# Rank-scatter of rows: early loads as one DMA of 10 KB packets, and two more thin groups

## The chip, the cores and the metric

The kernel runs on one core of one Trainium2 chip. The metric is device microseconds (us) of one execution. The record numbers the chip of each batch of experiments: chip 1 for the first batch (here B1), chip 9 for the second (B2), chip 2 for the last (C). The chip of the first comparison isn't recorded (here "chip A"; it could be one of the others). Three of the four first runs of the kernel before, and its trace, were taken earlier and stand under A too.

## The reference

```python
B, N, D = 8, 2048, 2560          # x: [B, N, D] float32 (168 MB), scores: [B, N] float32
order = np.argsort(scores, axis=1)
ranks = np.argsort(order, axis=1)
out[b_idx, ranks, :] = x         # row i of batch b goes to row ranks[b, i]
```

Each row of 10 KB is moved once, unchanged. The work is to find the ranks (a little arithmetic) and to move 168 MB in and 168 MB out.

## The kernel before

Ranks are counted on VectorE. The rows are cut into groups of 256 (128 partitions x 2 rows). Most groups are loaded to SBUF and scattered to their ranks by GpSimd's indirect DMAs, both on queue q0. Six groups (the first of batches 0 to 5) go another way: SP and ACT issue, per row, one DMA from DRAM to DRAM whose 10 KB go as 16 packets of 640 bytes ("row copies", queues q1 and q10; the trace of before has 25216 such packets for 1576 rows).

A "thin" group takes 4 partitions out of a group: their rows are made out of bounds for the scatter (by adding N to their rank), sometimes for the load too, and go by row copies. One DMA engine serves the four at 48-51, so a thin group there lightens that engine.

```python
GROUPS = [(256 * i, 2) for i in range(8)]
BULK = [(b, g) for b in range(B) for g in range(len(GROUPS)) if g or b not in DIRECT]   # 58 buffers
NBUF, LAG = 8, 4
THIN = {**{(b, 4): 48 for b in range(1, B, 2)}, (7, 5): 44}   # (batch, group): first partition
THIN_LOADS = [k for k in THIN if k[0]]
HALVED = range(34)                                             # loads split into 10 KB packets

def load(line, k, sem):
    ...   # a thin load: indirect DMA in which 4 partitions are out of bounds
    rows = x[b, r:r + P * m, :].rearrange("(p j) d -> p (j d)", j=m)
    for j in range(m if k in HALVED else 1):
        part = slice(j * D, (j + 1) * D) if k in HALVED else slice(0, m * D)
        line.eng.dma_start(out=xb[k % NBUF][:, part], in_=rows[:, part]).then_inc(sem, 16)
...
# row copies, 16 to a loop on SP and on ACT:
for i in range(G):
    line.eng.dma_start(out=out_bytes[bass.ds(at[i], ROW)],
                       in_=x_bytes[bass.ds(q * (G * ROW) + (first + i) * ROW, ROW)]).then_inc(s_rows[line], 16)
...
# GpSimd's loop:
for k, (b, g) in enumerate(BULK):
    if k >= LAG and k + NBUF - LAG < len(BULK):
        scatters_done(pl, k - LAG)          # the buffer is free
        load_ahead(k + NBUF - LAG)
    pl.wait(*loaded[k])
    pl.after(dve, t_bulk[b, g])             # the ranks are there
    for j in range(GROUPS[g][1]):
        scatter(k, j)                       # one indirect DMA per column: 128 rows
```

Of the kernel before, what the change touches and what calls it, by code (L numbers as in the profile page):

```python
# [40 lines left out]
def kernel(  # L41
# [6 lines left out]
    nc = tc.nc  # L48
# [18 lines left out]



    THIN = {**{(b, 4): 48 for b in range(1, B, 2)}, (7, 5): 44}  # L70
    HOLES = sorted(set(THIN.values()))

    THIN_LOADS = [k for k in THIN if k[0]]

    HALVED = range(34)

    STEPS = [(0, 1), (1, 2), (2, 4), (4, 8)]

# [16 lines left out]
    hole = pool.tile([P, len(HOLES)], F32, name="hole")  # L95
    below = pool.tile([P, 1], F32, name="below")
    thin_row = pool.tile([P, len(HOLES)], I32, name="thin_row")
    thin_i = {k: pool.tile([1, 4 * MMAX], I32, name=f"thin_i{k[0]}_{k[1]}") for k in THIN}
    rows_i = {b: pool.tile([1, WIDE], I32, name=f"rows_i{b}") for b in DIRECT}
    xb = [pool.tile([P, MMAX * D], F32, name=f"x{i}") for i in range(NBUF)]  # L100
    ps_col = psum.tile([P, 512], F32, name="ps_col")
# [7 lines left out]
    with tc.tile_critical(no_gpsimd_drain=True):  # L109
# [5 lines left out]
        s_scores = nc.alloc_semaphore("scores")  # L115
        s_first = nc.alloc_semaphore("first")
        s_load = [nc.alloc_semaphore(f"load{i}") for i in range(NBUF)]
        s_scat = [
            [nc.alloc_semaphore(f"scat{i}_{j}") for j in range(MMAX)]
            for i in range(NBUF)  # L120
        ]
        s_rows = {sp: nc.alloc_semaphore("rows_sp"), act: nc.alloc_semaphore("rows_act")}
        n_scat = [[0] * MMAX for _ in range(NBUF)]

        n_load = [0] * NBUF
        t_thin = []
# [1 line left out]
        def load(line, k, sem):  # L128
            b, g = BULK[k]
            r, m = GROUPS[g]  # L130
            if (b, g) in THIN_LOADS:

                i = HOLES.index(THIN[b, g])
                line.after(dve, t_thin[0])
                nc.gpsimd.indirect_dma_start(  # L135
                    out=xb[k % NBUF][:, :m * D],
                    out_offset=None,
                    in_=x.rearrange("b (q j) d -> (b q) (j d)", j=m),
                    in_offset=bass.IndirectOffsetOnAxis(ap=thin_row[:, i:i + 1], axis=0),
                    element_offset=(b * N + r) * D,  # L140
                    bounds_check=P - 1,
                    oob_is_err=False,
                ).then_inc(sem, 16)
                n_load[k % NBUF] += 1
                return
            rows = x[b, r:r + P * m, :].rearrange("(p j) d -> p (j d)", j=m)
            for j in range(m if k in HALVED else 1):
                part = slice(j * D, (j + 1) * D) if k in HALVED else slice(0, m * D)
                line.eng.dma_start(  # L149
                    out=xb[k % NBUF][:, part], in_=rows[:, part]  # L150
                ).then_inc(sem, 16)
                if k:
                    n_load[k % NBUF] += 1


        sp.eng.dma_start(out=s_in[:], in_=scores).then_inc(s_scores, 16)
        load(sp, 0, s_first)
        loaded = {0: (s_first, 16 * (2 if 0 in HALVED else 1))}


        t_zero = pl.did(nc.gpsimd.memset(ident[:], 0.0))
# [88 lines left out]
        def ranks(b, g_lo, g_hi):  # L250

            for g in range(g_lo, g_hi):
                lo = first_col(g)
                m = GROUPS[g][1]
                for j in range(m):
                    col = b * C + lo + j
                    score = s_col[:, lo + j, b:b + 1]
                    dve.after(dve, dve.n)

                    def count(i, lo_c, hi_c, do, **how):  # L260
                        dve.did(
                            do(  # L262
                                out=trash[i][:, :P * (hi_c - lo_c)],
                                in0=s_all[:, P * lo_c:P * hi_c],
                                accum_out=acc[i][:, col:col + 1],
                                **how,
                            )
                        )

                    count(  # L270
                        0, lo, C, nc.vector.tensor_scalar,
                        scalar1=score, scalar2=None, op0=OP.is_lt, op1=OP.add,
                    )
                    if lo:
                        count(
                            1, 0, lo, nc.vector.tensor_scalar,
                            scalar1=score, scalar2=None, op0=OP.is_le, op1=OP.add,
                        )
                    count(
                        2, lo, lo + m, nc.vector.scalar_tensor_tensor,  # L280
                        scalar=score,
                        in1=mask[:, MMAX - j:MMAX - j + m, :].rearrange("p a b -> p (a b)"),
                        op0=OP.is_equal, op1=OP.mult,
                    )
            cols = slice(b * C + first_col(g_lo), b * C + first_col(g_hi))
            dve.after(dve, dve.n)
            dve.did(
                nc.vector.tensor_tensor(  # L288
                    out=rank[:, cols], in0=acc[0][:, cols], in1=acc[1][:, cols], op=OP.add
                )  # L290
            )
            dve.after(dve, dve.n)
            dve.did(
                nc.vector.tensor_tensor(  # L294
                    out=rank[:, cols], in0=rank[:, cols], in1=acc[2][:, cols], op=OP.add
                )
            )
            dve.after(dve, dve.n)
            tick = dve.did(
                nc.vector.tensor_copy(out=rank_i[:, cols], in_=rank[:, cols])  # L300
            )
            for g in range(g_lo, g_hi):
                t_bulk[b, g] = tick
                if (b, g) in THIN:
                    cols = slice(b * C + first_col(g), b * C + first_col(g + 1))
                    i = HOLES.index(THIN[b, g])
                    dve.after(dve, dve.n)
                    t_bulk[b, g] = dve.did(
                        nc.vector.tensor_scalar(  # L309
                            out=rank_i[:, cols],  # L310
                            in0=rank[:, cols],
                            scalar1=hole[:, i:i + 1],
                            scalar2=None,
                            op0=OP.add,
                        )
                    )
# [11 lines left out]
                )  # L328

        def thin_to_bytes(b, g):  # L330
            m = GROUPS[g][1]
            dve.after(pe, pe.n)
            t_rows[b, g] = dve.did(
                nc.vector.tensor_scalar(  # L334
                    out=thin_i[b, g][:].rearrange("o (j i) -> o j i", j=m),
                    in0=ps_row[:1, :P * m].rearrange("o (j p) -> o j p", j=m)[
                        :, :, THIN[b, g]:THIN[b, g] + 4
                    ],
                    scalar1=float(b * N),
                    scalar2=float(ROW),  # L340
                    op0=OP.add,
                    op1=OP.mult,
                )
            )
# [63 lines left out]
        def thin_rows(n, b, g):  # L408
            line, name = ((sp, ENG.SP), (act, ENG.Activation))[n % 2]
            r, m = GROUPS[g]  # L410
            line.after(dve, t_rows[b, g])
            _, at = nc.values_load_multi_w_load_instructions(
                thin_i[b, g][:],
                engines=[name],
                min_val=b * N * ROW,
                max_val=(b * N + N - 1) * ROW,
                skip_runtime_bounds_check_because=(
                    "a rank counts other scores of one batch of N, so it lies in 0..N-1"
                ),
            )  # L420
            for i in range(4 * m):
                row = b * N + r + (THIN[b, g] + i % 4) * m + i // 4
                line.eng.dma_start(
                    out=out_bytes[bass.ds(at[i], ROW)],
                    in_=x_bytes[bass.ds(row * ROW, ROW)],
                ).then_inc(s_rows[line], 16)
                n_rows[line] += 1
# [37 lines left out]


        def scatters_done(line, k):
            i = k % NBUF
            for j in range(GROUPS[BULK[k][1]][1]):
                line.wait(s_scat[i][j], 16 * n_scat[i][j])  # L470

        def scatter(k, j):
            b, g = BULK[k]
            col = b * C + first_col(g) + j
            n_scat[k % NBUF][j] += 1
            nc.gpsimd.indirect_dma_start(  # L476
                out=out_flat,
                out_offset=bass.IndirectOffsetOnAxis(ap=rank_i[:, col:col + 1], axis=0),
                in_=xb[k % NBUF][:, j * D:(j + 1) * D],
                in_offset=None,  # L480
                element_offset=b * N * D,
                **(dict(bounds_check=N - 1, oob_is_err=False) if (b, g) in THIN else {}),
            ).then_inc(s_scat[k % NBUF][j], 16)

        def load_ahead(k):
            i = k % NBUF
# [47 lines left out]
```

## Time and profile before

| | before |
|---|---|
| median of 4 runs (chip A) | 772.09 us (770.55 to 772.5) |
| span of the profiled run | 769.8 us |
| VectorE / GpSimd / TensorE busy | 52% / 22% / 4% |
| bytes in DMA packets, mean rate | 319.74 MB, 415 GB/s |
| q0 packets, share of 16 engines | 29376, 92.0% |
| row copies (SP / ACT) | 792 / 784 |

A share of "16 engines" is the time that the packets of a queue took, over 16 times the span. The lines themselves are in the prediction below. One more view of before, the waits of SP's own queue:

```profile
SPq L109 <- DMA out_dram<-in_x_dram: 27.7, 1, 27.7
...
SPq L109 <- POOLq L109: 11.1, 1, 11.1
```

The columns are total us, number of waits, longest. The first is SP's wait, after it has issued its last row copy, until all its copies have landed. The second is how long SP then waits for GpSimd, thus for the scatters. Read the second as the slack of SP's row copies: they are done 11.1 us before the rest.

### The profile page before, as it was taken

What the parts mean: (1) busy time and instruction counts of PE and PEld (TensorE: products, weight loads), DVE (VectorE), ACT (ScalarE), POOL (GpSimd) and SP (SyncE); (2) the same over time, 40 slices, a digit from 0 to 9 for tenths busy, and PEclk for the clock granted to TensorE, in tenths of its full rate; (3) what the DMA queues carried; (4) which work ended last, traced back from release to release, by engine and by line L of the source; (5) the groups of instructions that cost most, each with busy time, mean ns of one, the idle gap of its engine ahead of it and who ended that gap; (6) DMA issues with size and microseconds to landing.
All of it is one profiled execution on the core that took longest, in us unless ns stands there. A gap on an engine that the chain in (4) does not pass through costs nothing.

```text
span 769.8 us, 8160 instructions
## 1 busy us (share of the span) xinstructions
PE 33.4 (4%) x166; PEld 29.2 (4%) x166; DVE 400.1 (52%) x824; ACT 0.0 (0%) x1; POOL 167.1 (22%) x213
## 2 busy tenths in 40 slices
PE   4000020020020020110000000000000000000000
PEld 4000010010010010110000000000000000000000
DVE  5999979999979999899999200000000000000000
ACT  0000000000000000000000000000000000000000
POOL 4114214312213131221212121212112121312100
PEclk8555555555555555565555555555555555555555
DMA  8999999999999999999999999999999999999997
GB/s 356 420 419 418 418 421 417 417 419 419 418 417 417 416 419 417 419 419 418 417 418 418 425 417 423 417 422 419 422 417 423 419 420 422 419 425 416 426 411 332
DMA packets 80130, 319.74 MB, mean 415 GB/s; under 512 B 28580, under 2 KB 53796, under 8 KB 53796
## 3 DMA queue, kind: packets, MB, share of 16 engines
q0 software_dynamic: 29376, 300.66, 92.0%
q1 hardware_dynamic: 25648, 10.85, 5.2%
q10 hardware_dynamic: 25088, 8.08, 4.2%
q14 instruction: 17, 0.14, 0.0%
q8 instruction: 1, 0.02, 0.0%
HBM read 168.25 MB, written 168.18 MB: 437 GB/s over the span
## 4 chain that ended last, share of the span: by engine, by line
DMA 63%; DVE 13%; another core or an unknown queue 10%; POOL 6%; issue 4%; PE 1%; POOLq 0%; SPq 0%
DMA out_dram<-x,rank_i 57%; DVE trash L262 12%; DMA x<-in_x_dram 6%; POOL out_dram L476 4%; POOL x L149 2%; DVE s_all L384 0%; POOL x L135 0%; PE ps_all L219 0%; DMA s_in<-in_scores_dram 0%; PE ps_col L198 0%; DVE rank_i L300 0%; DVE rank L294 0%; DVE rank L288 0%; PE ps_row L323 0%
## 5 line engine op out<-in xcount | busy, mean ns | idle before, releaser
L262 DVE TENSOR_SCALAR_CACHE_REDUCE trash<-s_all,s_col 128x1792 bf16<-128x1792 f32 (+7 forms) x240 | 315.2, 1348 | 4.6
L476 POOL DMA_INDIRECT out_dram<-x,rank_i x116 | 113.4, 978 | 135.8 <-issue 34.3
L149 POOL DMA_DIRECT2D x<-in_x_dram x83 | 46.7, 564 | 393.3 <-DMA out_dram<-x,rank_i 391.3
L262 DVE SCALAR_TENSOR_TENSOR trash<-s_all,s_col,mask 128x256 bf16<-128x256 f32 x128 | 61.5, 481 | 0.0
L219 PE MATMUL ps_all<-ident,s_col 128*128 128x128 f32 x128 | 27.2, 400 | 3.2 <-DVE s_all L384 2.8
L219 PEld LDWEIGHTS ps_all<-ident,s_col 128*128 128x128 f32 x128 | 26.0, 219 | 4.1 <-DVE s_all L384 3.1
L323 PE MATMUL ps_row<-ident,rank 128*1 128x128 f32 x22 | 5.9, 365 | 388.7 <-DVE rank_i L309 281.5
L384 DVE COPY s_all<-ps_all 128x512 f32<-128x512 f32 x32 | 20.6, 687 | 3.2 <-PE ps_all L219 2.8
L262 DVE DVE_READ_ACCUMULATOR trash<-s_all,s_col 128x1 f32 x240 | 19.9, 83 | 0.0
L323 PEld LDWEIGHTS ps_row<-ident,rank 128*1 128x1 f32 x22 | 1.3, 86 | 391.5 <-DVE rank_i L309 282.8
L135 POOL DMA_INDIRECT x<-in_x_dram,thin_row x5 | 5.2, 1031 | 43.9 <-DMA out_dram<-x,rank_i 40.3
L262 DVE DVE_READ_ACCUMULATOR trash<-s_all,s_col,mask 128x1 f32 x128 | 10.7, 83 | 0.0
L334 DVE TENSOR_SCALAR thin_i<-ps_row 1x8 int32<-1x8 f32 x5 | 0.8, 153 | 10.2 <-PE ps_row L323 10.2
L349 DVE TENSOR_SCALAR rows_i<-ps_row 1x256 int32<-1x256 f32 x6 | 2.5, 412 | 4.1 <-PE ps_row L323 4.1
L206 DVE COPY s_col<-ps_col 128x128 f32<-128x128 f32 x1 | 0.3, 292 | 4.5 <-PE ps_col L198 4.5
L198 PE MATMUL ps_col<-ident,s_in 8*128 8x8 f32 x16 | 2.1, 262 | 3.7 <-DMA s_in<-in_scores_dram 3.7
L198 PEld LDWEIGHTS ps_col<-ident,s_in 8*128 8x128 f32 x16 | 2.0, 211 | 3.7 <-DMA s_in<-in_scores_dram 3.7
L300 DVE CAST rank_i<-rank 128x16 int32<-128x16 f32 (+3 forms) x11 | 1.9, 173 | 0.4
L294 DVE TENSOR_TENSOR rank<-rank,acc 128x16 f32<-128x16 f32 (+3 forms) x11 | 1.9, 171 | 0.4
L288 DVE TENSOR_TENSOR rank<-acc,acc 128x16 f32<-128x16 f32 (+3 forms) x11 | 1.9, 170 | 0.4
L309 DVE TENSOR_SCALAR rank_i<-rank,hole 128x2 int32<-128x2 f32 x5 | 1.1, 229 | 0.2
L179 POOL TENSOR_SCALAR_AFFINE_SELECT mask<-mask 128x256 f32<-128x256 f32 x2 | 0.8, 396 | 0.0
(13 smaller groups left out, 2.5 us busy)
## 6 DMA issues: line engine op xcount, KB each, us to landing
x<-in_x_dram POOLq DMA_DIRECT2D x62, 1280.0 KB
x<-in_x_dram POOLq DMA_DIRECT2D x21, 2560.0 KB
out_dram<-in_x_dram SPq DMA_DIRECT2D x792, 10.0 KB
out_dram<-in_x_dram ACTq DMA_DIRECT2D x784, 10.0 KB
x<-in_x_dram SPq DMA_DIRECT2D x2, 1280.0 KB, 9.0
out_dram<-x,rank_i POOLq DMA_INDIRECT x116, 48.3
x<-in_x_dram,thin_row POOLq DMA_INDIRECT x5
s_in<-in_scores_dram SPq DMA_DIRECT2D x1, 64.0 KB
```

Source lines behind the costliest of these rows:

```text
L135: nc.gpsimd.indirect_dma_start(out=xb[k % NBUF][:, :m * D], out_offset=None, in_=x.rearrange("b (q j) d -> (b q) (j d)", j=m), in_offset=b ...
L149: line.eng.dma_start(out=xb[k % NBUF][:, part], in_=rows[:, part]).then_inc(sem, 16)
L198: nc.tensor.transpose(out=ps_col[:, B * c:B * (c + 1)], in_=s_in[:, r + j:r + m * P:m], identity=ident[:B, :B],)
L219: nc.tensor.transpose(out=ps_all[:, P * c:P * (c + 1)], in_=s_col[:, c, b:b + 1].to_broadcast([P, P]), identity=ident[:],)
L262: do(out=trash[i][:, :P * (hi_c - lo_c)], in0=s_all[:, P * lo_c:P * hi_c], accum_out=acc[i][:, col:col + 1], **how,)
L288: nc.vector.tensor_tensor(out=rank[:, cols], in0=acc[0][:, cols], in1=acc[1][:, cols], op=OP.add)
L294: nc.vector.tensor_tensor(out=rank[:, cols], in0=rank[:, cols], in1=acc[2][:, cols], op=OP.add)
L300: nc.vector.tensor_copy(out=rank_i[:, cols], in_=rank[:, cols])
L323: nc.tensor.transpose(out=ps_row[:1, P * j:P * (j + 1)], in_=rank[:, col:col + 1], identity=ident[:],)
L349: nc.vector.tensor_scalar(out=rows_i[b][:].rearrange("o (p j) -> o p j", p=P), in0=ps_row[:1, :WIDE].rearrange("o (j p) -> o p j", p=P), s ...
L384: nc.vector.tensor_copy(out=s_all[:, 512 * q:512 * (q + 1)], in_=ps_all[:, 512 * q:512 * (q + 1)],)
L476: nc.gpsimd.indirect_dma_start(out=out_flat, out_offset=bass.IndirectOffsetOnAxis(ap=rank_i[:, col:col + 1], axis=0), in_=xb[k % NBUF][:, ...
```

## The change

Its intent: fewer DMAs and completions for the loads, row copies of a few more rows to even out the engines, and two more split loads so that those copies get their turns.

```diff
-    THIN = {**{(b, 4): 48 for b in range(1, B, 2)}, (7, 5): 44}
+    THIN = {(1, 4): 48, (3, 4): 48, (4, 4): 48, (5, 4): 48, (6, 4): 36, (7, 4): 48, (7, 5): 44}
+    THIN_COLS = {k: 1 if k == (4, 4) else 2 for k in THIN}
-    THIN_LOADS = [k for k in THIN if k[0]]
-    HALVED = range(34)
+    THIN_LOADS = [(1, 4), (3, 4), (5, 4), (7, 4), (7, 5)]
+    HALVED = range(36)
 ...
-            for j in range(m if k in HALVED else 1):
-                part = slice(j * D, (j + 1) * D) if k in HALVED else slice(0, m * D)
-                line.eng.dma_start(
-                    out=xb[k % NBUF][:, part], in_=rows[:, part]
-                ).then_inc(sem, 16)
+            line.eng.dma_start(
+                out=xb[k % NBUF][:, :m * D],
+                in_=rows,
+                max_dma_last_dim=ROW if k in HALVED else None,
+            ).then_inc(sem, 16)
 ...      (one scatter semaphore per buffer in place of one per column; narrower index tiles;
           bounds checks on the thin columns alone)
```

More of the change, by code (lines that the diff above doesn't have):

```diff
@@ L97 @@
     thin_row = pool.tile([P, len(HOLES)], I32, name="thin_row")
-    thin_i = {k: pool.tile([1, 4 * MMAX], I32, name=f"thin_i{k[0]}_{k[1]}") for k in THIN}
+    thin_i = {k: pool.tile([1, 4 * THIN_COLS[k]], I32, name=f"thin_i{k[0]}_{k[1]}") for k in THIN}
     rows_i = {b: pool.tile([1, WIDE], I32, name=f"rows_i{b}") for b in DIRECT}
@@ L117 @@
         s_load = [nc.alloc_semaphore(f"load{i}") for i in range(NBUF)]
-        s_scat = [
-            [nc.alloc_semaphore(f"scat{i}_{j}") for j in range(MMAX)]
-            for i in range(NBUF)
-        ]
+        s_scat = [nc.alloc_semaphore(f"scat{i}") for i in range(NBUF)]
         s_rows = {sp: nc.alloc_semaphore("rows_sp"), act: nc.alloc_semaphore("rows_act")}
-        n_scat = [[0] * MMAX for _ in range(NBUF)]
+        n_scat = [0] * NBUF
         n_load = [0] * NBUF
@@ L146, in load @@
             rows = x[b, r:r + P * m, :].rearrange("(p j) d -> p (j d)", j=m)
-            for j in range(m if k in HALVED else 1):
-                part = slice(j * D, (j + 1) * D) if k in HALVED else slice(0, m * D)
-                line.eng.dma_start(
-                    out=xb[k % NBUF][:, part], in_=rows[:, part]
-                ).then_inc(sem, 16)
-                if k:
-                    n_load[k % NBUF] += 1
+            line.eng.dma_start(
[3 more added lines that the diff above has]
+            ).then_inc(sem, 16)
+            if k:
+                n_load[k % NBUF] += 1
         sp.eng.dma_start(out=s_in[:], in_=scores).then_inc(s_scores, 16)
         load(sp, 0, s_first)
-        loaded = {0: (s_first, 16 * (2 if 0 in HALVED else 1))}
+        loaded = {0: (s_first, 16)}
         t_zero = pl.did(nc.gpsimd.memset(ident[:], 0.0))
@@ L304, in ranks @@
                 if (b, g) in THIN:
-                    cols = slice(b * C + first_col(g), b * C + first_col(g + 1))
+                    cols = slice(b * C + first_col(g), b * C + first_col(g) + THIN_COLS[b, g])
                     i = HOLES.index(THIN[b, g])
@@ L330, in thin_to_bytes @@
         def thin_to_bytes(b, g):
-            m = GROUPS[g][1]
+            m = THIN_COLS[b, g]
             dve.after(pe, pe.n)
@@ L420, in thin_rows @@
             )
-            for i in range(4 * m):
+            for i in range(4 * THIN_COLS[b, g]):
                 row = b * N + r + (THIN[b, g] + i % 4) * m + i // 4
@@ L467, in scatters_done @@
         def scatters_done(line, k):
-            i = k % NBUF
-            for j in range(GROUPS[BULK[k][1]][1]):
-                line.wait(s_scat[i][j], 16 * n_scat[i][j])
+            line.wait(s_scat[k % NBUF], 16 * n_scat[k % NBUF])
         def scatter(k, j):
@@ L474, in scatter @@
             col = b * C + first_col(g) + j
-            n_scat[k % NBUF][j] += 1
+            n_scat[k % NBUF] += 1
             nc.gpsimd.indirect_dma_start(
@@ L481, in scatter @@
                 element_offset=b * N * D,
-                **(dict(bounds_check=N - 1, oob_is_err=False) if (b, g) in THIN else {}),
-            ).then_inc(s_scat[k % NBUF][j], 16)
+                **(dict(bounds_check=N - 1, oob_is_err=False) if j < THIN_COLS.get((b, g), 0) else {}),
+            ).then_inc(s_scat[k % NBUF], 16)
         def load_ahead(k):
```

## The prediction

> **What bounds the kernel now.** I read the page's busy rows first. VectorE is busy for 52% of the span and only up to slice 23 of 40, GpSimd for 22%, TensorE for 4%; the DMA row stands at 9 from the second slice to the last but one. So I read the queues and then the busy time by stretches:
>
> ```profile
> DMA  8999999999999999999999999999999999999997
> ...
> q0 software_dynamic: 29376, 300.66, 92.0%
> q1 hardware_dynamic: 25648, 10.85, 5.2%
> q10 hardware_dynamic: 25088, 8.08, 4.2%
> ```
>
> q0 carries what GpSimd issues (loads of x into SBUF, rank scatters out of it), q1 and q10 the copies of single rows from DRAM to DRAM that SP and ACT issue. 92.0 + 5.2 + 4.2 = 101.4% of 16 engines' span: the packets of an engine overlap by a little, and no engine rests. By stretch (the last two figures are the DMA share and GB/s):
>
> ```profile
> 0.00:20.00 20.00, 8.87 (x50) 8.20 (x50) 12.26 (x26) 0.02 (x1) 9.32 (x23) 0.83 0.89 359
> 20.00:100.00 80.00, 0.00 (x0) 0.00 (x0) 78.69 (x168) 0.00 (x0) 18.05 (x21) 0.52 1.02 419
> 500.00:600.00 100.00, 0.00 (x0) 0.00 (x0) 0.00 (x0) 0.00 (x0) 18.05 (x22) 0.50 1.02 421
> 765.00:769.00 4.00, 0.00 (x0) 0.00 (x0) 0.00 (x0) 0.00 (x0) 0.00 (x0) 0.50 0.16 67
> ```
>
> From 20 us on the share is 1.02 everywhere, with VectorE busy (20:100) or quite idle (500:600). When I count the packets in flight, there are at least 16 of them nearly always between 20 and 764 us. GpSimd's longest wait confirms it:
>
> ```profile
> POOL x L149 <- DMA out_dram<-x,rank_i: 391.3, 43, 11.1
> ```
>
> 391.3 us in 43 waits for scatters to land before their buffer is loaded again. That is the sign of a full queue: a scatter takes a median of 48.3 us from issue to landing, because so much is queued ahead of it. **The bound is therefore the sum of the packet times on the busiest DMA engine**, plus some 2 us of start and 2 us of end. The chain of waits puts 57% on scatters and 12% on the VectorE rank counts, but the counts lie beside loads already queued, and cutting them would free no engine.
>
> The end shows how evenly the engines are loaded. The DMA view for 755 to 770 us in 40 slices of 0.375 us:
>
> ```profile
> GB/s 423 420 451 433 439 410 437 410 437 410 437 437 437 410 437 437 437 437 437 410 437 437 437 437 410 382 328 273 109 82 55 55 27 27 0 0 0 0 0 0
> ```
>
> One engine is 437/16 = 27.3 GB/s. After 764 us about 15, 14, 12, 10, 4, 3, 2, 2, 1, 1 engines are still at work: 64 engine-slices. Sixteen equal engines would need 64/16 = 4 slices and not 10, so perfect balance is worth 6 x 0.375 = 2.25 us. **That is the most that rebalancing can give: 0.3%.**
>
> [...] The trace names no engines. It does show that of the 16 completions of a scatter one comes up to 6 us late and that this lag drops in steps near the thin groups. It also shows slow 10 KB scatter packets (mostly 400 to 440 ns, not 385) in runs of about 16, once per buffer, mostly one at a time: one engine that is some 3% slow, as the thin groups' place suggests.
>
> [...] The trace agrees closely in the stretch from 440 to 740 us, where all three queues are backed up:
>
> ```profile
> q0 software_dynamic: 9905, 119.68, 93.6%
> q1 hardware_dynamic: 9906, 3.19, 4.2%
> q10 hardware_dynamic: 9905, 3.19, 4.2%
> ```
>
> One packet each per turn, and the 4-byte completions count as turns. From 20 to 430 us the counts are 17457 to 14373: there the row copies are held by their issue (0.9 us a row in the trace), not by their turn. So the size of a load's packets matters only to how fast row copies get through.
>
> [...]
>
> **The change, part by part.** Packet times from the trace's packet records of the kernel before: 10 KB in or out of SBUF 385 ns, 20 KB 761 ns, 640 B (a sixteenth of a row copy) 32 ns, a 4-byte completion 9 ns.
>
> 1. *One DMA in place of two per early load.* 32 direct loads were halved (34 less the two thin ones among them), 31 of them on q0. One completion per engine goes for each: 31 x 9 = -0.28 us per engine. The data packets stay 10 KB if the limit of 10,240 is bytes, as the change's wording says. GpSimd issues some 31 DMAs of 0.56 us less, but may take longer for each; it is busy for 22%, so that is worth nothing on the path.
> 2. *Loads 34 and 35 go from 20 KB to 10 KB packets.* 8 partitions per engine x 2 loads x (2 x 385 - 761 = 9 ns) = +0.14 us per engine. They give the row copies more turns for two more buffers, some 26 us: at 0.90 in place of 0.97 us a row, about 2 rows more per queue.
> 3. *Thin group (4,4), one column at 48-51.* 4 rows are not scattered: engine 4 loses 4 x 385 = -1.54 us. They are still loaded.
> 4. *Thin group (6,4), two columns at 36-39.* 8 rows not scattered: engine 1 loses 8 x 385 = -3.08 us. Also still loaded.
> 5. *Their 12 row copies.* Each puts 32 + 9 = 41 ns on each engine: 12 x 41 = +0.49 us per engine. SP gets 4 more rows (796), ACT 8 more (792).
> 6. *One semaphore per buffer for the scatters, narrower index tiles, bounds checks only on thin columns, a third hole on VectorE.* Both columns were waited for before, and still are. The small VectorE work, well under a microsecond, lies where engines are full anyway. Nothing.
>
> Sum: -0.28 + 0.14 + 0.49 = +0.35 us on an ordinary engine; engine 4: 0.35 - 1.54 = -1.19; engine 1: 0.35 - 3.08 = -2.73. The mean over 16 is (14 x 0.35 - 1.19 - 2.73)/16 = +0.06 us: **the change moves hardly any work away; it only moves it between engines.**
>
> The end then depends on which engines are last. From the last scatter's completions, relative to their median, the last four are at +2.7, +1.7, +0.9, +0.6 us. I take the one at 2.7 to be engine 4, since its lag grew again between its relief points. It goes to 1.5. If the second is engine 1, the third (0.9 + 0.35 = 1.3) and engine 4 at 1.5 set the end: a gain of 1.2 us. If it is not, 1.7 + 0.35 = 2.05 sets it: 0.65 us. If neither laggard is relieved: 0.35 us lost. I take a gain of 0.9 us, of 772.13: **771.2 us**.
>
> **The rivals.**
> - *The row copies become the end.* At present q10's last packet is at 752 us, q1's at 757, while q0 ends at 768. With 0.97 us a row, ACT gains 8 - 2 rows (+5.8 us, so 758), SP 4 - 2 (+1.9, so 759). That stays 5 us or more ahead of q0's end. Only if the single-DMA loads gave the copies far fewer turns would they pass 766: in the early stage a buffer now has 35 q0 packets per engine against 36, and needs some 29 at the issue-held rate, so no. If it did happen: +2 to +8 us.
> - *The three-level pattern (partition, half, column) is dealt to the engines otherwise than the two-level one.* [...] The trace cannot speak against it, as it has no such load. Cost: if those loads ran 10% slower, 34 x 6.2 us of load x 0.1 = 21 us, 2.7%. If the limit were elements and not bytes, packets would be 20 KB from the start: the copies fall back to 0.97 us a row from the beginning; 796 x 0.97 + 23 = 795 us, 3% slower.
> - *The start gets better or worse.* In the first 20 us 2.2 us of engine time is lost (0.89 of 20). It is lost before the first packet, and the first load's first packet does not depend on its form. At most 0.3 us either way.
> - *Hidden anyway.* GpSimd's saved issue time is off the path (391 us of waiting absorbs it). I count on this.
>
> **Range and chances.** The three runs before span 770.55 to 772.5, so 1 us either way is noise. With the cases above from -2.25 (perfect balance) to +0.35 and that noise: 768.8 to 773.0. Faster by over 2% would need 15 us less in engines that have 4 us to lose: 0.01. Slower by over 2% needs one of the two bad readings of the new pattern: 0.03. Within 2%: 0.96.
>
> **What would show it.** Right: q0 with about 31 x 16 - 12 x 1 + 2 x 128 = 252 fewer packets (496 completions and 12 row scatters fewer, 256 from the two split loads more, so 29376 - 252 = 29124); the DMA share still 1.02 from 20 to 760 us; the last slices of GB/s falling from 437 to 0 in fewer steps; both copy queues done by 760 us. Wrong: a 10 KB packet of over 385 ns in the first 430 us[...], 20 KB packets there (limit in elements), copies still running after 764 us, or an end with one engine trailing by 3 us or more (the wrong engine was relieved).

All its packet times (385, 761, 32 and 9 ns) are medians of the trace. "Nearly always" 16 packets in flight is 99.9% of the time from 20 to 764 us. Four notes:

- The engine numbers, here and in the expectations, are only names: engine 1 is the one of partitions 36-39, engine 2 of 40-43, engine 3 of 44-47, engine 4 of 48-51. That these are four different engines was an assumption. The runs show a part of it: all_at_40 that 40-43 and 48-51 are on different ones, g32_e3 the same for 44-47 and 48-51 (one engine is early, at 763.4 us, and that of 48-51 last, at 770.0). That 36-39 are on one engine shows in the changed kernel's trace: near 645 us, when (6,4) is scattered, one chain of packets has four of 10 KB and five of 4 bytes in a row, the four skipped rows and a completion. "Some 3% slow" is 2.6% by the records of before: what the q0 packets of 394 to 464 ns took over 385 sums to 19.6 us from 20 to 764 us, if all of them are that engine's.
- "The trace agrees closely" can be read as the counts below it, and the order of the packets says the same. From 440 to 740 us, of 14118 pairs of packets of which one can be seen to follow the other on an engine, 14115 go from q0 to q1, from q1 to q10 or from q10 to q0. 0.97 us a row is 300 us for the 309.5 rows that q1 moved then.
- "41 ns on each engine" for a row copy: on one engine a 640-byte piece (32 ns) and a 4-byte completion (9 ns) of q1 take turns, in 1941 of 1971 pairs of before from 500 to 560 us.
- The 10% in the second rival is an assumption; the 6.2 us are 16 packets of 385 ns.

## The result

On chip A the changed kernel took 770.33 us (median of 4, 769.87 to 770.57) against 772.09: 1.76 us less. A ratio is the mean time of one kernel's fast runs over that of the other's in the same rounds, so it isn't quite the ratio of the medians: 0.998, 95% interval 0.9963 to 0.9997. (In the batches below the recorded ratios fit the runs only if the profiled run is left out; it matters for loads_only, whose seven runs would give 1.0022 and not 1.0006.) Executions over 1.5% slower than the fastest of the same kernel are left out of the means.

The queues of the changed kernel (packets, MB, share of 16 engines), and the stretches of the prediction that carry the argument:

```profile
q0 software_dynamic: 29136, 300.53, 92.2%
q1 hardware_dynamic: 25760, 10.89, 5.2%
q10 hardware_dynamic: 25344, 8.16, 4.2%
```

```profile
20.00:100.00 80.00, 0.30 (x3) 0.06 (x1) 78.69 (x168) 0.00 (x0) 16.95 (x18) 0.52 1.02 419
500.00:600.00 100.00, 0.00 (x0) 0.00 (x0) 0.00 (x0) 0.00 (x0) 18.14 (x22) 0.50 1.02 421
765.00:769.00 4.00, 0.00 (x0) 0.00 (x0) 0.00 (x0) 0.00 (x0) 0.00 (x0) 0.50 0.15 61
```

The shares are those of before to a hundredth: the bound is the same and is as full as it was. GpSimd still waits for scatters:

```profile
POOL x L146 <- DMA out_dram<-x,rank_i: 358.6, 38, 10.8
```

What differs is the end. The GB/s of the DMA view from 755 to 768.1 us, in 40 slices of 0.33 us:

```profile
GB/s 387 516 393 455 424 321 485 452 422 481 330 354 516 418 454 389 358 448 485 420 450 358 385 516 420 454 377 346 469 469 375 250 219 94 31 0 0 0 0 0
```

From 469 to 0 in six slices (2.0 us); before, the fall took eleven slices of 0.375 us (4.1 us). (A packet counts in the slice where it starts, and 394 packets of row copies are still among the 885; so the earlier slices swing.) From the packet records I worked out when each engine moved its last scatter packet, by pairing each engine's completions, which lie one scatter apart. The 16 ends:

| | first | mean | last | last minus mean |
|---|---|---|---|---|
| before, chip A | 764.7 | 765.76 | 768.1 | 2.35 us |
| changed, chip A | 765.0 | 765.76 | 766.5 | 0.78 us |

**The mean end hasn't moved; the last engine came 1.6 us nearer to it.** That is the gain in the profiled pair (span 769.8 to 768.1 us). And one thing got worse:

```profile
SPq L111 <- DMA out_dram<-in_x_dram: 15.0, 1, 15.0
SPq L111 <- POOLq L111: 2.3, 1, 2.3
```

SP's row copies now have a slack of 2.3 us and not 11.1.

### The profile page after: what moved, and what is told of

Its sections match the earlier page's. It is cut to its first block, busy times and chain, and to the rows that moved or that the text cites. A ratio compares the mean times of both kernels' runs of the same rounds, so it can differ in the third digit from the quotient of the medians.

```text
span 768.1 us, 8117 instructions
## 1 busy us (share of the span) xinstructions
PE 36.3 (5%) x170; PEld 30.6 (4%) x170; DVE 401.0 (52%) x829; ACT 0.0 (0%) x1; POOL 155.1 (20%) x182
## 3 DMA queue, kind: packets, MB, share of 16 engines
q0 software_dynamic: 29136, 300.53, 92.2%
## 4 chain that ended last, share of the span: by engine, by line
DMA 44%; another core or an unknown queue 19%; DVE 13%; issue 10%; POOL 9%; PE 1%; POOLq 0%; SPq 0%
DMA out_dram<-x,rank_i 38%; DVE trash L261 12%; POOL out_dram L473 7%; DMA x<-in_x_dram 6%; POOL x L146 2%; PE ps_all L218 0%; DVE s_all L383 0%; DMA s_in<-in_scores_dram 0%; POOL x L134 0%; PE ps_col L197 0%; DVE rank_i L299 0%; DVE rank L293 0%; DVE rank L287 0%; PE ps_row L322 0%
## 5 line engine op out<-in xcount | busy, mean ns | idle before, releaser
L146 POOL DMA_DIRECT2D x<-in_x_dram x52 | 35.3, 679 | 398.9 <-DMA out_dram<-x,rank_i 358.6
L322 PE MATMUL ps_row<-ident,rank 128*1 128x128 f32 x26 | 7.8, 402 | 392.3 <-DVE rank_i L308 184.8
L308 DVE TENSOR_SCALAR rank_i<-rank,hole 128x2 int32<-128x2 f32 (+1 forms) x7 | 1.8, 255 | 0.2
```

What stands on the lines that cost most here:

```text
L146: line.eng.dma_start(out=xb[k % NBUF][:, :m * D], in_=rows, max_dma_last_dim=ROW if k in HALVED else None,).then_inc(sem, 16)
L322: nc.tensor.transpose(out=ps_row[:1, P * j:P * (j + 1)], in_=rank[:, col:col + 1], identity=ident[:],)
```

## The experiments

The first theory: the gain is balance of the engines, from the thin groups, and the single DMAs give 0.3 us at most. The rivals: the single DMAs are the gain; or the wrong engine is named. A second question came from the traces of the first batch: executions above 773 us, and whether the row copies make them.

The table has each profiled execution but those of all_at_40 and halved_0, which are told below. "Last scatter" is the last engine's end and "minus mean" is that end less the mean of 16; "rows by 430" is how many row copies SP had issued at 430 us; "copies end" is q1's last packet.

| kernel (chip) | profiled run us | last scatter | minus mean | rows by 430 | copies end |
|---|---|---|---|---|---|
| before (A) | 771.55 | 768.1 | 2.35 | 456 | 757.0 |
| changed (A) | 769.87 | 766.5 | 0.78 | 447 | 764.3 |
| after_again (B1) | 775.54 | 768.3 | 2.38 | 430 | 770.9 |
| loads_only (B1) | 781.1 | 767.9 | 2.77 | 424 | 777.7 |
| thin_only (B1) | 772.16 | 768.7 | 2.63 | 456 | 759.5 |
| moved_40 (B1) | 773.26 | 767.8 | 2.07 | 433 | 768.1 |
| before_again (B2) | 771.42 | 767.7 | 1.85 | 448 | 763.4 |
| loads_only_2 (B2) | 771.54 | 768.1 | 2.38 | 450 | 761.9 |
| g32 (C) | 770.82 | 767.5 | 1.05 | 457 | 754.4 |
| g32_e4 (C) | 771.24 | 767.9 | 1.56 | 456 | 763.7 |
| g32_e3 (C) | 773.56 | 770.1 | 2.96 | 446 | 769.3 |
| g32_e34 (C) | 774.37 | 768.0 | 1.83 | 439 | 771.0 |

### after_again: the changed kernel in another batch

No edit.

> The changed kernel once more, for its noise and beside the other three on one chip. Theory (the gain is balance: the mean end of the 16 engines is unmoved at 765.8 us in both traces, only the last engine comes nearer to it): 770.3 us, about 1.7 us below the kernel before, last engine within 1 us of the mean.

Measured: 771.47 us (median of 6, 770.96 to 775.54) against 771.71 for before, ratio 0.9993 (0.998 to 1.0006). The expected 1.7 us are not there. In the trace one engine trails the mean by 2.38 us again, as in the kernel before on chip A. So the evenness of the changed kernel's end on chip A isn't a property of the kernel alone. The profiled run (775.54 us) was the slowest of the six, so by itself it doesn't explain the median, but thin_only below has the same thin groups, ran at 772.16 us and has an engine 2.63 us behind. In the slow run the row copies outlast the scatters. The DMA view from 764 to 780 us in slices of 0.4 us:

```profile
GB/s 439 429 407 325 223 146 64 53 26 53 5 42 11 15 14 11 21 5 0 0 0 0 0 0 0 0 0 0 0 0 0 0 0 0 0 0 0 0 0 0
...
q0 software_dynamic: 86, 0.71, 10.6%
q1 hardware_dynamic: 504, 0.16, 4.6%
q10 hardware_dynamic: 157, 0.05, 1.2%
```

After 768 us only 5 to 50 GB/s flow. These are 640-byte pieces of q1, on for another 3 us.

### loads_only: of the change the single DMAs alone

```diff
-    THIN = {(1, 4): 48, (3, 4): 48, (4, 4): 48, (5, 4): 48, (6, 4): 36, (7, 4): 48, (7, 5): 44}
-    HALVED = range(36)
+    THIN = {(1, 4): 48, (3, 4): 48, (5, 4): 48, (7, 4): 48, (7, 5): 44}
+    HALVED = range(34)
```

> The changed kernel with the thin groups of before and 34 split loads: of the change only the single-DMA loads. Theory (balance): 31 completions of 9 ns fewer per engine, so 0.3 us less, 771.8 us, and one engine still trailing the mean of the engines by about 2.3 us. Rival (the single DMAs are the gain, through fewer completions and less issue on GpSimd): 770.3 us.

Measured: 771.95 us (median of 7, 771.43 to 781.1), ratio 1.0006 (0.9994 to 1.0018). The rival's 770.3 us is out. The theory's trailing engine is there (2.77 us); its 0.3 us is below what the runs can tell. The mean end is 765.12 us against 765.82 in before_again and 765.76 on chip A, which has the sign of the fewer completions; but the second trace of this kernel (loads_only_2) has 765.7, so nothing is shown by it.

The profiled run took 781.1 us, and SP's waits show the cause:

```profile
SPq L111 <- DMA out_dram<-in_x_dram: 1.3, 1, 1.3
```

The line "SPq <- POOLq" is gone: SP never waited for GpSimd. It issued its last row copy at 776 us, 8 us after the last scatter packet.

### thin_only: of the change the thin groups alone

```diff
-            line.eng.dma_start(
-                out=xb[k % NBUF][:, :m * D], in_=rows,
-                max_dma_last_dim=ROW if k in HALVED else None,
-            ).then_inc(sem, 16)
+            for j in range(m if k in HALVED else 1):          # as before
+                part = slice(j * D, (j + 1) * D) if k in HALVED else slice(0, m * D)
+                line.eng.dma_start(out=xb[k % NBUF][:, part], in_=rows[:, part]).then_inc(sem, 16)
-    HALVED = range(36)
+    HALVED = range(34)
```

> The changed kernel with its early loads as two DMAs of half the columns, 34 of them: of the change only the two thin groups (and the shared semaphores). Theory (balance): most of the gain, 770.6 to 770.9 us, last engine within 1 us of the mean. Rival (the single DMAs are the gain): 772.1 us.

Measured: 772.01 us (median of 5, 771.7 to 772.21), ratio 1.0002 (0.999 to 1.0015). A miss for the theory: the thin groups alone gave nothing on this chip. The end of its trace (755 to 770 us, slices of 0.375 us):

```profile
GB/s 430 439 406 437 357 437 449 451 423 418 425 411 437 382 437 437 437 410 410 410 437 437 410 437 437 437 410 355 246 109 55 27 27 27 27 27 0 0 0 0
```

Five slices of 27 GB/s: a single engine works for 1.9 us when all others are done. The two groups had relieved engines, but not by enough the one that was last (it is the engine of partitions 48-51, as the section on moved_40 shows).

### moved_40: the relief of (6,4) on another engine

```diff
-    (6, 4): 36
+    (6, 4): 40
```

> The changed kernel with the thin group (6,4) at partitions 40-43 in place of 36-39: the same 8 rows fewer scattered[...]. Theory (engine 1 was the last one of before; no engine of the changed kernel ends before 765.0, so the one relieved by 2.7 us must have ended after 767.7): the gain is lost, 771.9 to 772.3 us, one engine ends about 2.7 us early (near 762.7) and one at about 768.1 again. Rival, as the prediction had it (engine 4 was the last one, its relief made the gain): 770.3 us as in the changed kernel, with one engine early and none late.

Measured: 771.83 us (median of 6, 771.11 to 774.04), ratio 1.0004 (0.9992 to 1.0016), no different from after_again beside it. In the trace one engine ends early, at 763.9 us, and two end late, at 767.6 and 767.8; after_again has one late (768.3) and the next at 766.7. That is roughly what moving 3 us from one engine to another does, but as a third engine is last either way, the time couldn't tell.

**Which engine is the last one can be read from the packet records.** In them a packet starts 3 or 4 ns before the one ahead of it on its engine ends (in 14097 of the 14118 pairs of before), so the records of the last 40 us fall into 16 chains, one for each engine. A scatter puts eight 10 KB packets on a chain, but four where a thin group leaves rows out. So the chain that lacks four packets in both scatters of (7,4), with six scatters to follow, is the engine of partitions 48-51. (Where two chains meet within nanoseconds, these counts decide which is which.) It ends at:

| trace | engine of 48-51 ends | last of the others |
|---|---|---|
| before (A) | 768.1 | 767.2 |
| changed (A) | 765.0, the first of all | 766.5 |
| after_again (B1) | 768.3 | 766.7 |
| thin_only (B1) | 768.7 | 766.9 |
| moved_40 (B1) | 767.8 | 767.6 |
| g32 (C) | 767.2 | 767.4 |

In loads_only, before_again, loads_only_2, halved_0 and g32_e3 it is the last one too. So the theory here is wrong for the kernel before: its last engine was that of 48-51 (the prediction's engine 4) and not engine 1. And **in the changed kernel's trace on chip A this engine ended 3.1 us earlier than before, where the change takes 1.2 us from it**. The rest is a matter of the execution. In the ten traces in which I looked, every 10 KB packet between 725 and 764 us that took 394 to 464 ns in place of 385 lies on this engine. If they are all its packets before that too, its slowness can be summed: what such packets took over 385 ns from 20 to 764 us is 16.8 us in the changed kernel on chip A and 20.5 us in thin_only, which has the same thin groups: 3.7 us apart, as are the two ends (765.0 and 768.7). In after_again it is 21.7 us. Why this engine is slow, and not always as slow, no run here shows.

### before_again and loads_only_2: is it the loads that slow the row copies?

In the first batch (B1) all three traces with single-DMA loads had SP behind (424 to 433 rows by 430 us), and the one with two DMAs did not (456). So I ran both forms again; the batch turned out to run on another chip (B2), where the expectations say "the chip of the experiments". before_again has no edit, loads_only_2 is loads_only unchanged.

> The kernel before, unchanged, for a trace on the chip of the experiments. In the four traces with single-DMA loads SP had issued 424 to 447 row copies by 430 us, in the two with two DMAs per load 456. Theory A (the single-DMA loads slow the issue of the row copies): at least 450 by 430 us, row copies done by 760 us, no run above 773 us. Theory B (slow issue is a matter of the single execution, whatever the loads): it may show here as well, under 445 rows and a run above 773 us.

> The changed kernel with the thin groups of before and 34 split loads, a second time, for another trace. Theory A (single-DMA loads slow the issue of row copies): under 445 rows on SP by 430 us again, row copies done after 764 us, profiled run above 773 us. Theory B (chance of the execution): may be 450 rows and 771.5 us.

Measured: before_again 771.74 us (771.42 to 772.02) with 448 rows by 430 us; loads_only_2 771.58 us (median of 4, with one run of 791.16) with 450. The runs of the kernel before beside them went up to 774.0 us. Theory A's figures fail: the kernel before had 448 rows and not 450, its row copies ended at 763.4 us, loads_only_2 had 450 and not under 445, and runs above 773 us come with either form of load. But the two batches ran on different chips, so 424 against 450 rows may be the chip as well as the execution. That **how fast SP issues row copies differs from execution to execution** is shown best on chip C below, where four traces with the same loops have 439 to 457 rows. A weaker form of theory A isn't excluded: over all traces with loops of 16, SP had 448 to 458 rows with two DMAs per load (four traces) and 424 to 450 with one (six), and on B1 five of 19 runs with single DMAs were above 773 us, none of 16 with two.

What sets the rate stays open. The issue times show where it is lost: up to 430 us, SP's pauses of over 1.5 us sum to 75.5 us in loads_only and 76.2 us in loads_only_2; the other gaps average 0.84 us and 0.79 us. From 30 to 430 us SP's issue is what holds the copies back, in the trace of before: mostly 3 to 6 rows, at no time 8, are issued and not yet moved. From 690 us to its last issue at 729 there are 29 to 34.

### all_at_40: is there a slow engine at all?

```diff
-    THIN = {**{(b, 4): 48 for b in range(1, B, 2)}, (7, 5): 44}      # the kernel before
+    THIN = {**{(b, 4): 40 for b in range(1, B, 2)}, (7, 5): 44}
```

> The kernel before with its four thin groups at partitions 40-43 in place of 48-51: the same rows go by row copies, but engine 2 is relieved and not engine 4. Theory (engine 4 is some 3% slow and the thin groups are there to make it even): engine 4 has 4 x (4 x 761 + 8 x 385 ns) = 24.5 us more to do and ends that much after the others, 792 to 796 us, 3% slower, its completions lagging by up to 25 us. Rival (where the relief lies is of no matter at this size): 771 to 774 us.

Measured: 792.38 us (792.29 and 792.46), ratio 1.0258 (1.0233 to 1.0282). The theory's size (two runs). The end of the trace, 760 to 791 us in slices of 0.775 us:

```profile
GB/s 424 411 385 424 437 411 424 330 50 26 26 40 26 26 26 26 26 26 26 26 26 26 26 26 26 26 26 26 26 26 26 26 26 26 26 26 26 0 0 0
```

26 GB/s is one engine (10,240 bytes in 385 ns are 26.6), and it works alone for 28 slices (22 us). So one engine has more to do than the others, the one that serves partitions 48-51, and the thin groups at 48 are worth 20 us. The relief of this engine is worth 2.6% here; the change only trimmed a remainder.

### halved_0: row copies late on purpose

```diff
-    HALVED = range(36)
+    HALVED = range(0)
```

> The changed kernel with no load split into 10 KB packets. All packets in flight are then 20 KB for loads, 34 x 8 x 9 ns = 2.4 us less work per engine, and row copies take 0.97 us each by their turns from the start, so some 33 per queue are left when the loads and scatters end; they are already issued and need 33 x 2 x 41 ns = 2.7 us of every engine. Theory (only the sum of packet times counts): 769 us, 2.4 us below the changed kernel on the same chip, row copies last. Rival of the prediction (the row copies become the end at their own pace, 3% slower): 780 to 795 us.

Measured: 782.12 us (781.34 to 782.67), ratio 1.0123 (1.0103 to 1.0143), 1.2% slower, clear of the noise. A miss for the theory, in one term. The scatters did end earlier on most engines (mean end 763.68 us, against 765.95 in after_again, on another chip: 2.3 us of the 2.4). But the row copies left over were dear. The DMA view from 764 to 781 us in slices of 0.43 us:

```profile
DMA  9999999999998987310000001000000000000000
GB/s 125 104 92 86 80 71 77 76 52 83 65 53 45 48 46 35 18 8 5 3 3 3 3 5 5 3 3 3 2 0 0 0 0 0 0 0 0 0 0 0
```

The engines are busy for 7 us more (nines) and yet move 45 to 125 GB/s. By the packet records a 640-byte piece takes 32 ns between 440 and 740 us, amid 10 and 20 KB packets, and 168 ns (q1) and 177 ns (q10) on average from 764 to 772 us, when some 600 of them are left almost by themselves (the last trickle in loads_only, after 768 us, takes 44 ns on average). **The sum of packet times is not conserved when small packets stand alone**; the rival of the prediction (the row copies become the end) is real, at 1.2% and not its 3%.

### g32, g32_e4, g32_e3, g32_e34: faster issue, and more relief

```diff
-    G = 16
+    G = 32                                  # g32: row copies, 32 to a loop
+    (2, 4): 48                              # g32_e4: g32 and this thin group, scatter only
+    (2, 4): 44                              # g32_e3: g32 and this one
+    (2, 4): 48, (2, 5): 44                  # g32_e34: g32 and both
```

> The changed kernel with the row copies' loops unrolled to 32 rows in place of 16, so that half of the 2 us breaks between loops go. Theory (the runs above 773 us of some executions are row copies issued late that outlast the scatters): SP has issued some 485 rows by 430 us, the row copies end by 745 us, and no run is above 773 us; the median stays within 0.5 us of the changed kernel on this chip (771.5), as the sum of packet times is the same. Rival (issue does not matter): the same median and as many runs above 773 us.

> As g32, with one more thin group that is loaded but not scattered, (2,4) at 48-51: 8 rows, 3.1 us off engine 4. In four traces of this chip one engine ends 1.9 to 2.6 us after the mean of all. If it is engine 4: 1.2 to 1.6 us below g32 and the last engine within 1.1 us of the mean. If it is another: as g32, +0.3 us for the 8 row copies (8 x 41 ns).

> As g32, with one more thin group, (2,4) at 44-47: 3.1 us off engine 3. If the last engine on this chip is engine 3: 1.2 to 1.6 us below g32. If it is another: as g32, +0.3 us.

> As g32, with both of these groups, engine 4 and engine 3 each relieved by 3.1 us. Whichever of the two is last: 1.0 to 1.5 us below g32, last engine within 1.1 us of the mean, about 769.9 us and the best of all. If the last is neither: +0.6 us over g32.

These ran on chip C, which isn't the chip that the expectations call "this chip" and compare with. There nine fast runs of the kernel before had a median of 772.82 us and went from 770.74 to 776.7 us; two more, of 783.25 and 786.84 us, count as slow. Measured, with the recorded ratio to it (the recorded ratios fit only if the run of 783.25 us is counted as fast; the means of the fast runs alone give 0.997 for g32 and g32_e4, and 1.001 to 1.002 for the other two):

| | median us | range | ratio (95%) |
|---|---|---|---|
| g32 | 771.28 | 770.62 to 772.02 | 0.9955 (0.9909 to 1.0002) |
| g32_e4 | 771.24 | 770.98 to 771.43 | 0.9953 (0.9906 to 0.9999) |
| g32_e3 | 773.2 | 772.36 to 782.35 | 0.9999 (0.9939 to 1.0059) |
| g32_e34 | 773.98 | 772.95 to 778.72 | 1.0 (0.9949 to 1.0051) |

The longer loops did less than expected: 457 rows by 430 us and not 485. There were fewer pauses of over 1.5 us between SP's issues, but they still sum to 70 us by then, against 74 us in before. In g32 the slack of SP's row copies was the largest of all traces but that of all_at_40 (22.8 us):

```profile
SPq L111 <- DMA out_dram<-in_x_dram: 28.0, 1, 28.0
...
SPq L111 <- POOLq L111: 13.1, 1, 13.1
```

None of 12 runs of g32 and g32_e4 is above 773 us, where four of the nine fast runs of the kernel before are. But g32_e3 and g32_e34 have the same loops and ran slow too, with row copies until 769 and 771 us. So the unrolled loops are not shown to be the cure; the two good kernels may have drawn good executions.

The reliefs did what a relief does, one engine each: in g32_e4 one engine (that of 48-51) ends at 763.4 us, 2.2 us ahead of the next, and in g32_e3 another likewise (763.4, the next 766.4). But they didn't bring the last end nearer: it stayed at 767.9 us or later. In g32_e4 and g32_e34 an engine that was given no more relief is last; in g32_e3 it is the engine of 48-51 again, at 770.0 us, where g32 with the same relief for it has 767.2. The times say the same: neither relief is below g32, as it would have been for the last engine. g32 is the best candidate that the runs point to; that it beats the changed kernel isn't shown, as the two never ran on one chip.

## Why the prediction was right, point by point

- **The bound** (the sum of packet times on the fullest engine): right. DMA share 1.02 in both traces; moving 24.5 us of packets onto one engine made the kernel 20 us longer (all_at_40).
- **Sum of work, +0.06 us on the mean engine**: right to the noise; the mean of the 16 ends is 765.76 us in both traces of chip A. That they agree to the hundredth is luck: over the traces of the table it goes from 765.1 to 767.1.
- **Packet count**: 29136 on q0, predicted 29124. The 12 missing are the 12 skipped rows: each still leaves a 4-byte packet of 9 ns. The same shows before: 3324 four-byte packets on q0 are 204 DMAs x 16 and 60 skipped pieces (40 rows of scatters, 20 pairs of rows of loads). In the changed kernel 2840 are 173 x 16 and 72. The error is 12 x 9/16 = 7 ns per engine.
- **Single DMAs worth nothing on the path, and dealt to the engines as before**: right; 10 KB packets kept their 385 ns (the median of 15350 on q0 from 20 to 430 us), where the chains of packets can be followed a single-DMA load puts 16 on each (200 to 216 us), and loads_only is at 1.0006.
- **The gain of 0.9 us**: right in sign and kind on chip A, 1.76 us in size, and in part by luck. The prediction took the engine at +2.7 us (+2.6 by the chains of packets) to be engine 4, and the chains show that it was. The term that was mis-sized is "It goes to 1.5": with 1.2 us taken off it was to be 1.5 us over the median and still last; in the changed kernel's trace it is the first to end, 3.1 us earlier than before, as far as one trace can tell because its packets were less slow in that execution (see moved_40). So another engine set the end, 0.8 us over the mean. The opposite happens too: in after_again and thin_only the same engine is last again, 2.4 and 2.6 us behind, and the gain of the changed kernel is 0.07% with an interval on both sides of zero. So the slow engine's lag is no constant to be tuned against. The honest size of the change over the batches is 0 to 0.2%.
- **Row copies done by 760 us**: wrong. The step was "ACT gains 8 - 2 rows (+5.8 us, so 758), SP 4 - 2 (+1.9, so 759)", with issue at 0.90 us a row. The issue rate was taken as fixed. It isn't: 447 rows by 430 us in the changed kernel, 424 to 458 over all. SP's copies ended at 764.3 us on chip A, so that the prediction's own sign of being wrong, "copies still running after 764 us", came up there; and in five executions of the table they ended between 768.1 and 777.7. All five took 773.3 us or more; the seven others took 772.2 or less. In four of the five (all but g32_e3, whose last scatter came at 770.1 us) the copies outlasted the scatters. So the first rival of the prediction happens. It is a matter of the execution at least in part (chip C); all five had single-DMA loads, but so had four of the seven others, and that the change makes it likelier is neither shown nor excluded.

## What to carry to other kernels

When all DMA engines are full from start to end, look at when each of them stops: only the last one's lag over the mean (here 2.35 us of 769.8) can be won by moving work between them, and one execution's lag is not another's: with the same thin groups the slow engine here ended at 765.0 us and at 768.7. Before a tune of a few tenths of a per cent is believed, run it in a second batch, on a second chip, beside the kernel before. And keep small background copies well ahead of the end: amid large packets a 640-byte piece costs 32 ns, in a crowd of its own kind some five times that on average (168 and 177 ns in halved_0), and their issue rate varies between executions (439 to 457 rows by 430 us in the four traces of chip C).
